# RWKV-7 layer of a two-layer trunk: one head per partition half, per-chunk transition matrices, a 16-wide inverse and LoRA inputs by linearity

## The chip, the cores and the metric

The kernel runs on one core of a Trainium2 chip. The metric is the device time of one execution in microseconds. The engines are TensorE (PE, with its weight loads PEld), VectorE (DVE), ScalarE (ACT), GpSimd (POOL) and SyncE (SP), which issues the DMAs.

## What is computed

A block of 512 tokens with 1024 channels goes through an RWKV-7 layer, an MLP, a differential-attention layer and a second MLP, each followed by a LayerNorm. Only the RWKV layer is touched by the change:

```python
xx = _token_shift(x) - x
xr, xw, xk, xv, xa, xg = (x + xx * mu[i] for i in range(6))   # written out in the source
r, k, v = xr @ w_r, xk @ w_k, xv @ w_v
w = -softplus(-(w0 + tanh(xw @ w1) @ w2)) - 0.5
a = sigmoid(a0 + (xa @ a1) @ a2)
g = sigmoid(xg @ g1) @ g2
kk = k * k_k;  kk = kk / max(norm(kk), 1e-12)                 # per head of 64
k = k * (1 + (a - 1) * k_a)
# per head, state S (64 x 64), 512 steps:
#   S_t = S_{t-1} diag(exp(-exp(w_t))) + (S_{t-1} a_t) b_t^T + v_t k_t^T ;  y_t = S_t r_t
y = _wkv7_scan(r, decay, k, v, -kk, kk * a)
y = layer_norm_per_head(y) + sum(r * k * r_k) * v
return (y * g) @ w_o
```

There are 16 heads of 64 channels. All data is float32.

## The kernel before

Dense products are made in three passes: each operand is split into a rounded high part (`split`, L101, a cast on ACT at L102) and a low part (a subtraction at L103, on POOL for the weights), and `mm3` (L134) multiplies high by high, high by low and low by high (L137 to L139). Weights come from DRAM in 256 KB pieces (`wst`).

The method `rwkv` first makes the LoRA inputs: DVE builds 24 mixed inputs (L262) from differences that POOL makes (L258), and PE multiplies them by the LoRA weights (L264). The mixed inputs of k, r and v follow in the same way (L245, L246). Then come the projections: k and r transposed, channels on partitions, with 512 columns, v with tokens on partitions and 256 columns. k also gives the squared norms (L300), whose inverse roots go through DRAM. The results go to DRAM and come back per pair of heads.

The sequence of 512 is cut into 8 chunks of 64. Heads are handled in 8 pairs p (128 channels) and 4 groups g of two pairs. For each pair `front` and `back` make decayed versions of r, k, a and b (the scan along time is L567; the products `ar` and `bk` are at L87, L599 and L600), and `amat` multiplies them into 64x128 blocks per chunk (L472), masks them on DVE (L474, L475) and transposes `bk` (L479). A triangular matrix of each chunk must be inverted: `inverse` writes the diagonal 32x32 blocks to DRAM (`nbD`), reads them back as `nu`, one block half on each partition (L503), and does a substitution of 31 steps with two operations each on DVE (L510 and L512; POOL for one group); the result goes out as `gbD` and comes back as `gt`. `inverse2` completes the 64x64 inverse with 32x32 matmuls (L535, L543). Then `chunk` runs 8 times for each of the 4 groups, and each run needs the state that the run before has left: 64x64 matmuls at L627 and L629, a copy, a product with the inverse (L632), a copy (L634), a product with the keys (L637), four scalings on DVE (L640), and products with the output matrix (L646). `finish` normalizes (L671 to L698), and the group's w_o product is added to the output rows (L407). A LayerNorm (L731 on; its transposes are L777) leads to the first MLP.

What runs when is set by three things: the `PLAN` string, which lists the steps of the RWKV layer in order (projections, F and B for front and back, A for `amat`, i and j for the inverse, s for a chunk, f for finish, w for w_o), priority offsets beside it (`PO`, `TP`), and the scheduler of the tile framework, which writes each engine's instructions in one order from this. DMAs are issued by SP in order. So the chunks of one group are woven with projections, the A blocks and the w_o products of others.

Of the kernel before, what the change touches and what calls it, by code (L numbers as in the profile page):

```python
# [8 lines left out]
F32 = mybir.dt.float32  # L9
# [9 lines left out]
P = 128  # L19
# [41 lines left out]
PO = {"k": [None, None, None, None], "r": [None, None, None, None], "v": [None, None, None, None], "F": [300, 300, 300, 300], "B": [300, 300, 300, 300], "A": [300, 300, 300, 300], "i": [600, 600, 600, 600], "j": [600, 600, 600, 600], "s": [0, 0, 0, 900], "f": [300, 300, 300, 1800], "l": [None, None, None, None], "c": [None, None, None, None], "w": [None, None, None, None], "n": [None, None, None, None]}  # L61
TP = {}


class Trunk:
# [102 lines left out]
    def rwkv(self):  # L168
# [5 lines left out]
        self.vD = self.t(self.dr, "vD", [T, D])  # L174
        self.rnD = self.t(self.dr, "rnD", [16, T])
        self.ssD = self.t(self.dr, "ssD", [4, 4, T])
        nbD = self.t(self.dr, "nbD", [4, 16, 4, 32, 32])
        gbD = self.t(self.dr, "gbD", [4, 16, 4, 32, 32])
        rp = self.pool("res", 1)
        self.psT = None  # L180
        with ExitStack() as ph:
            psA = self.pool("psA", 2, space=PSUM, ctx=ph)
            psE = self.pool("psE", 2, space=PSUM, ctx=ph)
            psB = self.pool("psB", 2, space=PSUM, ctx=ph)
            lp = self.pool("lora", 1, ctx=ph)
            ip = self.pool("inv", 1, ctx=ph)
            ep = self.pool("ew", 1, ctx=ph)
            ar_ = self.pool("arena", 4, ctx=ph)
            nbc = [0]
# [4 lines left out]
            xp = self.pool("xp", 1, side="right", ctx=xc)  # L194

            cvh = self.t(lp, "cvh", [P, 2, NK])
# [7 lines left out]
            self.rkb = self.t(lp, "rkb", [P, NK, 2])  # L204
# [7 lines left out]
            def big(tag, shape, dt=F32):  # L212
                if tag == "ba":
                    return self.t(rp, tag, shape, dt, bufs=4)
                if tag == "bc":
                    nbc[0] += 1
                    if nbc[0] % 4 in (1, 2):
                        return self.t(rp, "acc", shape, dt, bufs=2)
                    return self.t(ar_, "bc", shape, dt, bufs=2)
                return self.t(ar_, tag, shape, dt)  # L220

            l1 = big("ba", [P, NK, 256])
            lts = [big("ba", [P, 4, T]) for _ in range(2)]
            lts = [t[:, j] for t in lts for j in range(4)]
            xt = self.t(xp, "xt", [P, NK, T + 1])
            V.memset(xt[:, :, 0:1], 0.0)
            for c0, c1 in ((0, 1), (1, 2), (2, 4), (4, 6), (6, 8)):
                nc.sync.dma_start(out=xt[:, c0:c1, 1:T + 1], in_=a["xT"][:, c0:c1, :])
                nc.sync.dma_start(out=l1[:, c0:c1, :], in_=a["l1"][:, c0:c1, :])

            def mix(i, tag):
# [4 lines left out]
                for c in range(NK):  # L236
                    mix1(i, c, his[c], los[c], None, G if str(c) in (MRP if i == 0 else MVP) else V)
                return his, los

            def mix1(i, c, hi, lo, xx, E):  # L240
                tmp = self.t(xp, "tmp", [P, T], bufs=3)
                x0 = xt[:, c, 1:T + 1]
                if xx is None:
                    xx = tmp
                    G.tensor_tensor(out=xx, in0=xt[:, c, 0:T], in1=x0, op=ALU.subtract)  # L245
                V.scalar_tensor_tensor(out=tmp, in0=xx, scalar=cv[:, V_MU + i, c:c + 1], in1=x0, op0=ALU.mult, op1=ALU.add)  # L246
                self.split(hi, lo, tmp, E)

            pw = self.t(psB, "ch", [P, T])
            pa = self.t(psB, "ch", [P, T])  # L250
            pg = self.t(psB, "yy", [P, T])
            mk = [[big("bb", [P, 4, T], F32R) for _ in range(2)] for _ in range(2)]
            mk = [[z[c // 4][:, c % 4, :] for c in range(NK)] for z in mk]
            n = 0
            for c in range(NK):
                x0 = xt[:, c, 1:T + 1]
# [853 lines left out]
```

## Time and profile before

| | |
|---|---|
| median of three runs | 1532.91 us (1530.49 to 1537.92) |
| profiled execution, time | 1537.76 us |
| profiled execution, span | 1535.8 us |
| PE busy, share of the span | 92% |
| DVE, ACT, POOL busy | 54%, 37%, 28% |
| mean granted clock of PE | 0.931 |

The profile comes from one execution. A busy microsecond of PE is not one at full speed: the view of stretches gives the granted clock (PEclk) beside the busy time, 1.00 for 2.4 GHz and 0.5 for 1.2 GHz. The RWKV layer takes the first third of the span; the rest, two MLPs and the attention, is dense matmuls for the most part. The timelines give the start and the length of an instruction; a matmul in fp32 leaves two records, and a matmul's length includes its fill, so that starts of neighbours are nearer to each other than lengths.

### The profile page before, as it was taken

Reading aid. Unit: us, or ns where it says so; the run is one execution under the profiler, and the core shown is the slowest. Engines: PE = TensorE matmul, PEld = TensorE weight load, DVE = VectorE, ACT = ScalarE, POOL = GpSimd, SP = SyncE. Lnnn points to the kernel's source line nnn. Section 1 sums busy time; section 2 is a strip of 40 time slices with the busy share of each in tenths; the row PEclk is TensorE's granted clock in tenths of the full one; section 3 lists DMA queues with packets and bytes.
Section 4 is the critical chain, followed back from the end, with each engine's and each line's share of the span. In section 5 each row is a group of like instructions: output and inputs, shape, how many; then the busy total and the mean of one; then the engine's idle time right before and its main releaser. Section 6 shows DMA issues by size and latency. Waiting matters only on the chain.

```text
span 1535.8 us, 21834 instructions
## 1 busy us (share of the span) xinstructions
PE 1410.0 (92%) x8296; PEld 1151.9 (75%) x8296; DVE 829.9 (54%) x1668; ACT 561.0 (37%) x1074; POOL 430.6 (28%) x383
## 2 busy tenths in 40 slices
PE   7879888968899799999999989999988999999997
PEld 2547677847766598888888878888877988888886
DVE  8975475855876754333333553456667333333346
ACT  2333334143333362332314244566454413233220
POOL 5863333264335341010101144313232201010010
PEclk9889989755689999999999999999998999999999
DMA  5235463335131243333333035223112433333311
GB/s 163 69 125 146 122 146 103 97 77 132 54 96 42 96 138 111 96 96 97 97 99 93 28 102 158 76 76 110 62 64 74 138 96 96 96 96 96 96 42 55
DMA packets 89119, 148.14 MB, mean 96 GB/s; under 512 B 34312, under 2 KB 48040, under 8 KB 89016
## 3 DMA queue, kind: packets, MB, share of 16 engines
q1 hardware_dynamic: 89016, 146.76, 32.4%
q8 instruction: 65, 1.06, 0.3%
q14 instruction: 38, 0.31, 0.1%
HBM read 127.74 MB, written 10.57 MB: 90 GB/s over the span
## 4 chain that ended last, share of the span: by engine, by line
PE 72%; DVE 14%; DMA 7%; POOL 3%; ACT 2%; issue 2%; SPq 0%; DVEq 0%; ACTq 0%; POOLq 0%
PE a L137 11%; PE a L138 10%; PE a L139 10%; PE o L138 5%; PE o L139 5%; PE o L137 5%; PE s L138 5%; PE s L139 5%; PE s L137 5%; DMA nu<-nbD 3%; PE e L472 2%; DVE ba L262 1%; DMA gbD<-gu 1%; PE o L959 1%; DVE gtm L510 1%
## 5 line engine op out<-in xcount | busy, mean ns | idle before, releaser
L102 ACT CAST whi<-wst 128x1024 fp32r<-128x1024 f32 (+1 forms) x208 | 195.5, 952 | 354.8 <-PE a L139 146.4
L103 DVE TENSOR_TENSOR wlo<-wst,whi 128x1024 fp32r<-128x1024 f32 x120 | 149.6, 1247 | 223.7 <-ACT whi L102 223.7
L103 POOL TENSOR_TENSOR wlo<-wst,whi 128x512 fp32r<-128x512 f32 (+1 forms) x88 | 165.8, 1899 | 254.8 <-ACT whi L102 247.2
L87 POOL TENSOR_TENSOR r<-r 128x512 f32<-128x512 f32 x64 | 69.1, 1080 | 522.0 <-ACT hh L818 519.5
L137 PE MATMUL a<-ba,whi 128*128 128x512 f32 (+1 forms) x336 | 122.7, 366 | 2.7 <-DVE qT L907 2.2
L820 DVE TENSOR_TENSOR hl<-r,hh 128x512 fp32r<-128x512 f32 x64 | 45.8, 717 | 143.8 <-POOL r L87 143.8
L139 PE MATMUL a<-ba,wlo 128*128 128x512 f32 (+1 forms) x336 | 121.8, 363 | 0.0
L138 PE MATMUL a<-ba,whi 128*128 128x512 f32 (+1 forms) x336 | 121.7, 362 | 0.0
L139 PE MATMUL s<-ba,wlo 128*128 128x512 f32 (+1 forms) x232 | 81.3, 351 | 0.0
L138 PE MATMUL s<-ba,whi 128*128 128x512 f32 (+1 forms) x232 | 81.0, 349 | 0.0
L137 PE MATMUL s<-ba,whi 128*128 128x512 f32 (+1 forms) x232 | 80.8, 348 | 0.0
L137 PE MATMUL a<-whi,ba 128*128 128x256 f32 x256 | 76.0, 297 | 3.8 <-ACT ev L312 3.1
L138 PE MATMUL o<-ba,whi 128*128 128x512 f32 (+1 forms) x200 | 71.9, 359 | 3.6 <-DVE ba L103 3.6
L138 PE MATMUL a<-wlo,ba 128*128 128x256 f32 x256 | 74.9, 293 | 0.0
L137 PEld LDWEIGHTS a<-ba,whi 128*128 128x128 f32 x336 | 64.5, 193 | 13.7 <-issue 2.4
L139 PE MATMUL a<-whi,ba 128*128 128x256 f32 x256 | 74.5, 291 | 0.0
L137 PE MATMUL o<-ba,whi 128*128 128x512 f32 (+1 forms) x200 | 71.7, 359 | 1.3 <-ACT ba L102 1.3
L139 PE MATMUL o<-ba,wlo 128*128 128x512 f32 (+1 forms) x200 | 71.6, 358 | 0.0
L139 PEld LDWEIGHTS a<-ba,wlo 128*128 128x128 f32 x336 | 64.3, 192 | 9.5
L138 PEld LDWEIGHTS a<-ba,whi 128*128 128x128 f32 x336 | 64.6, 192 | 9.1
L137 PE MATMUL o<-whi,hh 128*128 128x512 f32 x176 | 68.7, 390 | 0.0
L138 PE MATMUL o<-wlo,hh 128*128 128x512 f32 x176 | 68.6, 390 | 0.0
(376 smaller groups left out, 3548.2 us busy)
## 6 DMA issues: line engine op xcount, KB each, us to landing
wst<-in_m SPq DMA_DIRECT2D x128, 512.0 KB, 3.9
wst<-in_kv SPq DMA_DIRECT2D x16, 512.0 KB, 3.8
wst<-in_wk SPq DMA_DIRECT2D x16, 256.0 KB, 4.2
wst<-in_wr SPq DMA_DIRECT2D x16, 256.0 KB, 3.4
wst<-in_wv SPq DMA_DIRECT2D x16, 256.0 KB, 3.8
wst<-in_q SPq DMA_DIRECT2D x8, 512.0 KB
kT<-kT SPq DMA_DIRECT2D x16, 256.0 KB, 3.3
wst<-in_wo SPq DMA_DIRECT2D x8, 512.0 KB, 3.3
```

Of the source, the lines that this page charges most:

```text
L87: return eng.tensor_tensor(out=out, in0=in0, in1=in1, op=ALU.mult)
L102: self.nc.scalar.copy(out=hi, in_=src)
L103: (lo_eng or self.nc.vector).tensor_tensor(out=lo, in0=src, in1=hi, op=ALU.subtract)
L137: mm(ps, lh, rh, start=first, stop=False)
L138: mm(ps, lh, rl, start=False, stop=False)
L139: mm(ps, ll, rh, start=False, stop=last)
L262: V.scalar_tensor_tensor(out=mx, in0=xx, scalar=cv[:, V_MU + i, c:c + 1], in1=x0, op0=ALU.mult, op1=ALU.add)
L472: PE.matmul(ps[:, c, :], d["bk"][hs, 4 * b + c].rearrange("p a t -> p (a t)"), d["ar"][hs, 4 * b + c].rearrange("p a t -> p (a t)"), start ...
L510: E.tensor_tensor(out=tmv, in0=GU[:, 0:m, s:s + 1].to_broadcast([P, m, n]), in1=NU[:, s:s + 1, s + 1:32].to_broadcast([P, m, n]), op=ALU.mult)
L820: V.tensor_tensor(out=hl, in0=r, in1=hh, op=ALU.subtract)
L959: PE.matmul(po[:, qb, :], at[:, kb, :], vt[:, kb, f * P:(f + 1) * P], start=(kb == 0), stop=(kb == qb))
```

## The change

The RWKV layer is rewritten; MLPs and attention stay.

- LoRA: the mixing is applied to the weights. POOL makes `ls = mu * l1` and `lx = l1 - ls` (three small products and one subtraction for each of 8 channel blocks), and PE adds `lx` times x and `ls` times the shifted x, two output blocks, 32 matmuls of 512 columns. The mixed inputs of k, r and v are made by ACT and DVE in PSUM.
- v is projected with channels on partitions like k and r. Norms are computed in two steps for eight heads each.
- The two heads of a pair lie on the two halves of the partitions (`H`). `amat` makes `am`, and copies `bn` and `an`.
- The inverse works on 16x16 blocks: 15 steps with two DVE operations, the 128 blocks of a group with one on each partition; `inverse2` widens them to 32 and 64 with 64x64 matmuls.
- `solve` makes for each chunk a transition matrix `mt` and an output matrix `rt` from the inverse, with six groups of sixteen 64x64 matmuls per pair.
- `scan` then carries the state: in each step one product `mt` times state is added in PSUM to a product that doesn't depend on the state, and DVE scales the sum into the next state.
- `finish` uses bn_stats for each chunk; the w_o step W(g) takes a whole group.
- The order is one string, without priority offsets. PSUM is 2 + 6 banks.

```diff
+PLAN = ("k0 r0 k1 r1 N0 k2 k3 N1 r2 r3 m v0 F0 A0 v1 F1 A1 v2 F2 v3 I0 x J0 J1 U0 U1 S0 A2 S1 F3 A3 Y0 Y1 "
+        "F4 I1 J2 J3 U2 U3 S2 A4 S3 F5 A5 Y2 Y3 W0 F6 I2 J4 J5 U4 U5 S4 A6 S5 F7 A7 Y4 Y5 W1 "
+        "I3 J6 J7 U6 U7 S6 S7 Y6 Y7 W2 W3")
...
+            def lora(c):
+                for i, c0, c1 in ((1, 0, 64), (4, 64, P), (5, P, 256)):
+                    G.tensor_scalar(out=ls[:, c, c0:c1], in0=l1[:, c, c0:c1], scalar1=cv[:, V_MU + i, c:c + 1],
+                                    scalar2=0.0, op0=ALU.mult, op1=ALU.add)
+                G.tensor_tensor(out=lx[:, c], in0=l1[:, c], in1=ls[:, c], op=ALU.subtract)
+                for ps, c0 in ((pwa, 0), (pg, P)):
+                    PE.matmul(ps, lx[:, c, c0:c0 + P], x0(c), start=(c == 0), stop=False)
+                    PE.matmul(ps, ls[:, c, c0:c0 + P], xs(c), start=False, stop=(c == NK - 1))
...
-                    PE.matmul(ps[r, :], l1[:, c, c0:c0 + r.stop - r.start], mx, start=(c == 0), stop=(c == NK - 1))
...
-        nc.sync.dma_start(out=NU.rearrange("p s t -> p (s t)"),
-                          in_=bass.AP(tensor=nb.tensor, offset=nb.offset, ap=[[0, 2], [1024, 64], [1, 1024]]))
-        for s in range(31):
-            n, m = 31 - s, s // 2 + 1
...
+        for q in range(2):
+            for h in range(2):
+                src = self.nbD[g, q, h]
+                r = 32 * (2 * q + h)
+                nc.sync.dma_start(out=NU[r:r + 32],
+                                  in_=bass.AP(tensor=src.tensor, offset=src.offset,
+                                              ap=[[16 * 65, 32], [64, 16], [1, 16]]))
+        for s in range(15):
+            n, m = 15 - s, s + 1
...
+        ps = self.bank((P, NCH, CH))
+        for c, h in HS:
+            PE.matmul(ps[H[h], c, :], w[H[h], c, :], bn[H[h], h, c, :], start=True, stop=True)
+        mt = self.t(cm, "mt", [P, NCH, CH], bufs=2)
+        V.tensor_tensor(out=mt, in0=ps, in1=cst[:, C_I2:C_I2 + CH].unsqueeze(1).to_broadcast([P, NCH, CH]), op=ALU.add)
...
+        for c in range(NCH):
+            ps = pc2[c % 2][:, c // 2, :]
+            if c < NCH - 1:
+                for h in range(2):
+                    PE.matmul(ps[H[h]], bn[:, h, c, :], uv[:, h, c, :], start=True, stop=(c == 0))
+            for h in range(2):
+                PE.matmul(py[H[h], c, :], am[:, h, c, 64:P], uv[:, h, c, :], start=True, stop=(c == 0))
+            if c:
+                if c < NCH - 1:
+                    for h in range(2):
+                        PE.matmul(ps[H[h]], mt[H[h], c, :], sc[H[h], c, :], start=False, stop=True)
+                for h in range(2):
+                    PE.matmul(py[H[h], c, :], rt[H[h], c, :], sc[H[h], c, :], start=False, stop=True)
+            if c < NCH - 1:
+                V.tensor_scalar_mul(sc[:, c + 1, :], ps, pc[:, c:c + 1])
...
-        for q, h in QH:
-            PE.matmul(ch[R[q], 0, h, :], ra[q][:, h, c, 0:CH], sv[q][:, h, :], start=True, stop=True)
-        for q, h in QH:
-            PE.matmul(yy[R[q], h, :], ra[q][:, h, c, CH:2 * CH], sv[q][:, h, :], start=(h == 0), stop=False)
-        S.copy(out=rs, in_=ch[:, 0])
-        for q, h in HQ:
-            PE.matmul(ch[R[q], 1, h, :], gf[R[q], 8 * h + c, :], rs[R[q], h, :], start=True, stop=True)
...
+        for c in range(NCH):
+            V.bn_stats(out=st[:, c, :], in_=py[:, c, :])
+            V.bn_aggr(out=mv[:, c, :], in_=st[:, c:c + 1, :])
```

The order on PE in the old chunk loop, in a stretch of group 1 (ch and yy are the PSUM tiles of the chunk, uv the values and state, acc, bc and bb its matrices, a the PSUM of another pair's A):

```order
L627 MATMUL ch_3313<-uv_3106,acc_1648 64x64
L629 MATMUL yy_3314<-uv_3106,acc_1648 64x64
L627 MATMUL ch_3313<-uv_3106,acc_1648 64x64
L629 MATMUL yy_3314<-uv_3106,acc_1648 64x64
L627 MATMUL ch_3313<-uv_3108,bc_1649 64x64
L629 MATMUL yy_3314<-uv_3108,bc_1649 64x64
L627 MATMUL ch_3313<-uv_3108,bc_1649 64x64
L629 MATMUL yy_3314<-uv_3108,bc_1649 64x64
L479 MATMUL a_2982<-cst_58,bk_2705 128x128 x4
L632 MATMUL ch_3313<-rs_3315,gf_2744 64x64 x4
L483 MATMUL a_2988<-rkb_112,r_484_2637 64x2 x8
```

The chunk's matmuls stood in small sets, woven with the A blocks of a later pair (L479, L483).

The order on PE where the new group 1 (pairs 2 and 3) begins its J and U (e is a PSUM bank, bb the A blocks `am`, tt the inverse, an and bc the copies of a, b and values):

```order
L528 MATMUL e_2607<-q_2605,bb_2112 64x64 x16
L534 MATMUL e_2626<-tt_2603,q_2624 64x64 x16
L541 MATMUL e_2646<-q_2644,bb_2112 64x32 x16
L548 MATMUL e_2665<-tt_2603,q_2663 32x32 x16
L528 MATMUL e_2691<-q_2689,bb_2291 64x64 x16
L534 MATMUL e_2710<-tt_2687,q_2708 64x64 x16
L541 MATMUL e_2730<-q_2728,bb_2291 64x32 x16
L548 MATMUL e_2749<-tt_2687,q_2747 32x32 x16
L564 MATMUL e_2770<-cst_58,vT_2768 64x64 x16
L569 MATMUL e_2789<-bc_2139,bb_2112 64x64
L574 MATMUL e_2808<-an_2177,tt_2603 64x64 x13
L569 MATMUL e_2789<-bc_2139,bb_2112 64x64 x15
```

The four J steps of one pair stand behind each other with no other row between, then those of the second pair, then U.

The order on DVE in the old inverse (gu is the inverse in the making, nu the block read back, t the decay sum of a front):

```order
L510 TENSOR_TENSOR gtm_1305<-gu_1280,nu_1282 128x96
L512 TENSOR_TENSOR gu_1280<-gu_1280,gtm_1305 128x4x24
L510 TENSOR_TENSOR gtm_1308<-gu_1280,nu_1282 128x115
L512 TENSOR_TENSOR gu_1280<-gu_1280,gtm_1308 128x5x23
L567 SCALAR_TENSOR_TENSOR t_270_1391<-cst_58,t_270_1391 128x512
L510 TENSOR_TENSOR gtm_1311<-gu_1280,nu_1282 128x110
L512 TENSOR_TENSOR gu_1280<-gu_1280,gtm_1311 128x5x22
L510 TENSOR_TENSOR gtm_1314<-gu_1280,nu_1282 128x126
```

And on DVE where the new inverse of group 1 begins (gr and gn belong to the finish of pair 0 or 1, nu is the block read back):

```order
L100 SCALAR_TENSOR_TENSOR gr_2454<-gr_2454,gv_2451 128x8
L101 SCALAR_TENSOR_TENSOR gr_2453<-gr_2454,gr_2453 128x8
L636 SCALAR_TENSOR_TENSOR gn_2465<-gmv_2434,gr_2453 128x8
L505 TENSOR_TENSOR gtm_2554<-gu_2548,nu_2547 128x15
L507 TENSOR_TENSOR gu_2548<-gu_2548,gtm_2554 128x15
L505 TENSOR_TENSOR gtm_2557<-gu_2548,nu_2547 128x28
L507 TENSOR_TENSOR gu_2548<-gu_2548,gtm_2557 128x2x14
L505 TENSOR_TENSOR gtm_2560<-gu_2548,nu_2547 128x39
L507 TENSOR_TENSOR gu_2548<-gu_2548,gtm_2560 128x3x13
```

The 31 steps of up to 136 columns have become 15 of up to 64, and they stand in DVE's order behind the statistics of both pairs of the group before.

## Rows read from the trace of the kernel before

**Rows 1.** PE's timeline, the first MLP: start us, us, instruction, its count, idle before.

```profile
531.52 0.28 PE L137 MATMUL s<-ba,whi 128*128 128x256 f32 x1
...
539.95 1.09 PE L777 MATMUL e<-cst,acc 128*128 128x128 f32 x4 [4.09 <-DVE lr L96]
```

**Rows 2.** Stretches: us; busy us (count) of PE, PEld, DVE, ACT, POOL; PEclk; DMA; GB/s.

```profile
250.00:300.00 50.00, 42.85 (x358) 36.15 (x357) 36.24 (x99) 12.51 (x31) 11.79 (x15) 0.84 0.38 105
300.00:350.00 50.00, 34.72 (x405) 27.97 (x403) 29.02 (x61) 20.63 (x46) 28.57 (x58) 0.62 0.28 68
350.00:400.00 50.00, 39.16 (x412) 33.36 (x412) 30.00 (x87) 14.31 (x38) 16.58 (x30) 0.52 0.40 104
...
450.00:500.00 50.00, 46.99 (x412) 33.74 (x410) 32.73 (x82) 17.42 (x46) 22.74 (x27) 0.99 0.14 40
```

**Rows 3.** PE's waits, 0 to 532 us: sum us, times, longest us.

```profile
PE e L300 <- ACT rnb L296: 13.9, 5, 7.6
```

**Rows 4.** The chain that ended last, longest pieces: start us, us, what.

```profile
166.08 14.53 DMA nu<-nbD
...
307.14 12.58 DMA gbD<-gu
...
359.65 3.21 DMA gbD<-gu
```

**Rows 5.** PE's timeline over one chunk step.

```profile
494.90 0.33 PE L627 MATMUL ch<-uv,bb 128*64 128x64 f32 x2
...
495.18 0.34 PE L627 MATMUL ch<-uv,bb 128*64 128x64 f32 x4
495.30 0.33 PE L629 MATMUL yy<-uv,bb 128*64 128x64 f32 x4
...
499.14 0.33 PE L627 MATMUL ch<-uv,bb 128*64 128x64 f32 x2
```

**Rows 6.** PE's groups of instructions, the LoRA matmuls: count, busy us, mean ns, idle.

```profile
L264 PE MATMUL ch<-ba,ba 128*64 128x512 f32 x32 | 16.6, 735 | 9.4 <-DVE ba L262 9.4
```

**Rows 7.** PE's timeline near 490 us, full clock.

```profile
490.13 0.45 PE L632 MATMUL ch<-rs,gf 64*64 64x64 f32 x8
490.50 0.50 PE L137 MATMUL a<-r,bc 128*128 128x512 f32 x1
...
491.31 0.39 PE L137 MATMUL a<-r,bc 128*128 128x512 f32 x1
491.54 0.39 PE L138 MATMUL a<-rnb,bc 128*128 128x512 f32 x1
```

**Rows 8.** PE's timeline near 363 us, half clock.

```profile
362.98 0.69 PE L632 MATMUL ch<-rs,gf 64*64 64x64 f32 x8
363.60 2.07 PE L472 MATMUL a<-ar,bk 64*128 64x128 f32 x8
```

**Rows 9.** DVE's groups of instructions, 0 to 532 us: busy us, mean ns, idle.

```profile
L640 DVE SCALAR_TENSOR_TENSOR uv<-ch,gpc,sps 64x64 f32<-64x64 f32 x96 | 23.6, 280 | 6.9 <-PE ch L637 3.4 <-PE yy L646 1.3 <-ACT bc L102 0.9
...
L567 DVE TENSOR_TENSOR_SCAN t<-cst,t 128x512 f32<-128x512 f32 x8 | 9.7, 1218 | 12.7 <-ACT t L566 12.7
...
L474 DVE TENSOR_TENSOR ba<-e,cst 64x512 f32<-64x512 f32 x8 | 5.5, 689 | 3.5 <-PE e L472 3.3
...
L672 DVE TENSOR_SCALAR gm<-gm 128x8 f32<-128x8 f32 x8 | 1.4, 186 | 0.1
```

**Rows 10.** ACT's groups of instructions, 0 to 532 us.

```profile
L480 ACT COPY bb<-e 128x512 f32<-128x512 f32 x4 | 2.4, 588 | 6.9 <-PE e L479 6.9
```

**Rows 11.** DVE's timeline in an inverse.

```profile
181.53 0.22 DVE L510 TENSOR_TENSOR gtm<-gu,nu 128x58 f32<-128x58 f32 x1
...
187.06 0.29 DVE L510 TENSOR_TENSOR gtm<-gu,nu 128x126 f32<-128x126 f32 x1
...
187.39 1.23 DVE L512 TENSOR_TENSOR gu<-gu,gtm 128x126 f32<-128x126 f32 x1
```

**Rows 12.** POOL's timeline in the same microseconds.

```profile
187.29 1.18 POOL L87 TENSOR_TENSOR ar<-rnb,e 128x512 f32<-128x512 f32 x1 [13.13 <-ACT e L571]
```

More of the change, by code (lines that the diff above doesn't have):

```diff
@@ L236, in mix @@
                 for c in range(NK):
-                    mix1(i, c, his[c], los[c], None, G if str(c) in (MRP if i == 0 else MVP) else V)
+                    mix1(i, c, his[c], los[c])
+                    if each is not None:
+                        each(c)
                 return his, los
[L240 to L247, printed above, removed]
@@ L344, in A @@
-            def A(p):
-                g, q = p // 2, p % 2
-                if q == 0:
-                    start(g)
-                gd = grp[g]
-                self.amat(pse, p, gd, el[p])
-                for half in range(2):
-                    r0 = 64 * q + 32 * half
-                    nc.sync.dma_start(out=nbD[g, :, 2 * q + half].rearrange("u s t -> s u t"),
-                                      in_=gd["ab"].rearrange("p h c t -> p (h c) t")[r0:r0 + 32, :, 32 * half:32 * half + 32])
@@ L355, in inv @@
-            def inv(g):
-                GU = self.t(ip, "gu", [P, 16, 32], bufs=2)
-                with tc.high_priority(offset=-(PO["i"][g] or 0)):
-                    nc.sync.dma_start(out=GU, in_=a["i32"])
-                self.inverse(ip, GU, nbD[g], gbD[g], G if str(g) in IPOOL else V)
-            def inv2(g):
-                self.inverse2(cm, ((psB, "ch"), (psB, "yy"), (psA, "a"), (psA, "a"))[g], gbD[g], grp[g])
-            pse = (psE, "e")
-            acc, wst, wos = [], {}, {}
-            def load(g):
-                if not acc:
+                nc.sync.dma_start(out=self.ssD[4 * g:4 * g + 4], in_=ss[0:4])
@@ L369, in load, with W @@
+            mr = mix(0, "bc")
+            el, tab = {}, {}
+            acc, wst = [], {}
+            def W(g):
+                if g == 0:
                     for i in range(2):
@@ L394, in wo @@
[L394 to L401 removed]
+                ws = []
@@ L402, in wo @@
+                for tt in range(NT):
                     for n in range(2):
@@ new lines, in inverse @@
+    def inverse(self, g):
+        nc, ep = self.nc, self.ep
+        V = nc.vector
+        NU = self.t(ep, "nu", [P, 16, 16])
+        GU = self.t(ep, "gu", [P, 16, 16])
+        nc.sync.dma_start(out=GU.rearrange("p s t -> p (s t)"), in_=self.a["i16"])
+        for q in range(2):
+            for h in range(2):
+                src = self.nbD[g, q, h]
[5 more added lines that the diff above has]
+            n, m = 15 - s, s + 1
+            tm = self.t(ep, "gtm", [P, 64], bufs=2)
+            tmv = tm[:, 0:m * n].rearrange("p (i t) -> p i t", t=n)
+            gv = GU[:, 0:m, s + 1:16]
+            V.tensor_tensor(out=tmv, in0=GU[:, 0:m, s:s + 1].to_broadcast([P, m, n]),
+                            in1=NU[:, s:s + 1, s + 1:16].to_broadcast([P, m, n]), op=ALU.mult)
+            V.tensor_tensor(out=gv, in0=gv, in1=tmv, op=ALU.add)
+        nc.sync.dma_start(out=self.gbD[g], in_=GU.rearrange("p s t -> p (s t)"))
```

682 lines of the change are left out of this document (310 added, 372 removed).

## The prediction, made before the changed kernel ran

> **What bounds the kernel now.** I read the table of stretches first, then TensorE's waits, then the chain that ended last, then single timelines for prices. The rest of the program, from the first MLP on, is the same code in both kernels, so only the time until the first MLP can run freely counts. In the kernel before, its first matmul starts at 531.52 us, but the engine later stands for 4.1 us until the last LayerNorm transposes at 539.95 [rows 1]; I count 541 us as the old end of the RWKV stage.
>
> TensorE is busy 35 to 47 us of every 50 in this stage [rows 2], but that hides two things. Between 300 and 400 us the granted clock is 0.62 and 0.52, so many of those busy microseconds are at the lower level, 1.2 GHz. And the engine rarely waits for long: the largest sum of waits at one line is 13.9 us, of L300 [rows 3]. The chain shows what stands behind that: the copy of the 32-wide blocks back from DRAM (`nu<-nbD`) takes 14.53 us, `gbD<-gu` 12.58 us [rows 4]. The old stage is a thread of latencies, filled rather well with projections and w_o matmuls of other groups. A chunk step of four heads starts at 494.90, the next at 499.14, 4.24 us, and there are 32 of these [rows 5].
>
> **The change part by part.**
>
> *LoRA and mixes.* Twenty-four mixed inputs vanish from DVE; in their place are 32 fp32 matmuls of 512 columns. One such matmul is two records; a record is 0.735 us long with its fill [rows 6], so a matmul lies between 0.735 and 1.47 us, and I take 0.95, as consecutive records overlap: 32 x 0.95 = 30 us, ending near 37 us. The old LoRA ended near the same place with projection matmuls already between, so this part gains little.
>
> *Projections.* Dense matmuls start 0.23 us apart [rows 7]. Twelve units of 48: 12 x 48 x 0.23 = 132 us. v now has 512 columns where it had 256, the same work. Norms 7 us, three fronts and two A-matrices between them 18 us, small waits 4: 37 + 132 + 7 + 18 + 4 = 198. The first inverse is mostly behind v2 and v3; with its last transfers J0 starts at 205.
>
> *Price of a group of sixteen 64x64 matmuls.* Eight records (four matmuls) of L632 occupy 490.13 to 490.50, 0.37 us [rows 7]; in a running stream four records start within 0.12 us (L627 at 495.18, the next at 495.30 [rows 5]), eight within 0.23, so sixteen matmuls take 0.37 + 3 x 0.23 = 1.06 us; 4 x 0.37 = 1.48 is the other bound. At the lower clock the eight take 362.98 to 363.60, 0.62 [rows 8], and sixteen, at twice 0.23 for each further eight, 2.0, 0.93 more. Of the 0.37, some 0.1 us stands beyond the 0.23 of the stream; it is paid where the work changes from dense tiles to quadrants. Some 100 such changes are 10 us if none is hidden; I count none of it, as the groups wait for DVE anyway. The Trainium skill ("TensorEngine Tiling (Array Packing)", Tiling Modes, Key Properties) says that a change of tiling mode drains the engine, which speaks against weaving 64x64 groups with other tiles; by that rule paid in full, the sum would be 10 us later, by the row's tenth it stays.
>
> *One pair's J.* Four groups (two only 32 columns wide), 4.0 us; on DVE a mask product and a sum from PSUM at 0.69 [rows 9] and a transpose at 0.7; an ACT copy at 0.59 [rows 10] and two half ones, 0.3 on the path; hops 0.3. Together 7.3, and the order has the pair's four groups in one row with nothing between, so two pairs take 14.6. *One pair's U.* Six groups, 6.4 us, with copies only partly covered by the parallel branch: 7 us, two pairs 14.
>
> *Scan, A, F, Y.* Here DVE sets the pace. Per group of two pairs: 14 scan scalings of 128x64 at 0.31 (a 64x64 from PSUM is 0.28 [rows 9]) 4.3; eight masks at 0.69 5.5; sixteen bn_stats at about 0.29 and sixteen bn_aggr at 0.2 7.8; two rsqrt chains, 24 small operations at 0.19 (128x8 is 0.186 [rows 9], which the bn_aggr follow too) 4.6; one front with its scan of 1.22 [rows 9] and five passes at 0.7 4.8. Sum 27.0; with the ramp of the first steps and hops 32 us. A scan step is short now (two PSUM accumulations, one DVE product), under 1 us against 4.24 for four heads before; but the group must wait for U and J first.
>
> *Inverse.* Thirty DVE operations of at most 64 elements at 0.24 (0.22 for 58 [rows 11]) 7.2 us, 2.8 more for a front's operations that stand between them in DVE's order. nbD out and back 4.5, gbD and dc 5. Bounds for the NU read, four transfers of 32 KB in 64-byte pieces: 1.6 us, half the 3.21 of gbD<-gu, which moves 128 KB, and 14.5, the old read [rows 4]; gbD<-gu, also many small pieces, is nearest, and I take 2.5. If it were the old one, +12 us for each of three groups. DVE work before and after the transfers, masks, products and transposes, adds 3.
>
> *One loop.* 14.6 + 14 + 32 + 4.5 + 7.2 + 2.8 + 5 + 3 = 83. W (48 dense matmuls, 11 us) lies in the idle time of the inverse. Three loops (groups 1 to 3), of which the last saves the A of a next group: 3 x 82 = 246.
>
> *Tail.* After U7: the scans 9, statistics and rsqrt of two pairs 12 (half of the 7.8 + 4.6 per pair is not enough: they follow each other), copies and transposes 5, W2 and W3 at 11 each, the LayerNorm of the last row blocks on DVE 14, and some 6 in which the first MLP weights' low parts stand behind LayerNorm operations in GpSimd's order: 68 us. *Removed without replacement:* the 14-us reads, the old chunk chain, the transposes of v.
>
> *Sum at full clock:* 205 + 29 (J0 to U1) + 246 + 68 = 548, against 541: +7. Two corrections. First, operations of DVE with two SBUF inputs stretch when GpSimd runs: beside a 1.18-us GpSimd operation the inverse's 128x126 took 1.23 instead of 0.29 [rows 11, 12]. About 3.5 us a group, 10 in all; the bounds are 0 and 10 for each group. The Trainium skill ("SBUF — State Buffer", Who interferes with whom) has a tensor_tensor with both inputs in SBUF contend with GpSimd's reads; by that rule, the trace agrees. Second, the clock. A loop holds twenty 64x64 groups with 0.93 each at stake, 18.6 us. In 250 to 300 us, a mix of dense and small work, the mean grant is 0.84, a third of the time at the lower level; in 300 to 400 it is 0.57, some 86% [rows 2]. The new group stage has less dense work than the former and more of it than the latter. I take a third, 6.2 a loop over three and a half loops, 22 us.
>
> So 548 + 10 + 22 = 580, 39 us later. The profiled execution is 1537.8 us, its span 1535.8 with 2 us around it: 1576.8. The median of the runs lies 4.9 us below the profiled one: **1572 us**.
>
> **The rivals.**
>
> *A: the loop is shorter, and the kernel faster.* If A and F of the next group finish under the first scan, so that NU's read and the inverse lie under the second scan and Y, a loop loses 12 us: 36 less. With the clock held and contention as taken, 541 - 548 + 36 - 10 = 19 us faster, 1514; with none of the contention 1504. For it: removed 14-us reads, and steps of under 1 us. Against: DVE carries 27 us in that stretch already, in one order.
>
> *B: the clock holds, the rest as forecast.* +17: 1550. For it: 450 to 500 us has 0.99 with chunk steps, though interleaved with dense matmuls [rows 2].
>
> *C: the clock stays low.* 86% of 18.6 over three and a half loops is 56, with the +17 a difference of 73 us: 1606. It decides from the point at which TensorE's busy share between inverses falls to that of 300 to 400 us. The Trainium skill ("TensorE: Matmul & The Clock Gate", What's actually happening) has activity release the lower level and idle bring it back; by that, C holds wherever the inverses leave TensorE idle, and 2.0 for 1.06 a group is what it costs.
>
> *D: about the same.* The +17 cancelled by 17 us of overlap that I don't see, 1533.
>
> **How the numbers follow.** Forecast 0.37, B 0.15, C 0.13, A 0.25, D 0.10. The range is 1508 to 1612, from the middle of A (half of its chance within) to C, with the NU read's upper bound partly outside. Half a per cent, 8 us, is about what a measurement of this kernel can tell from no change. Faster by more than that is 0.25 (A), within it 0.10 (D), slower 0.65 (the rest).
>
> **What would show it.** Right: in the new profile 64x64 groups at about 1.06 us at the full clock; J0 near 205, J2 near 290; first MLP matmuls near 580; a table of stretches in which TensorE is busy 25 to 35 us of 50 between 230 and 500 us with a grant of 0.7 to 0.9; DVE waiting some 3 us for NU. Wrong: a loop well under 75 us, inverse operations under scans, or a first MLP matmul before 530 (A); grants of 0.95 and more (B) or near 0.55 (C); a NU read of over 6 us. If matmuls of two partition halves don't run beside each other here as in the L632 rows, sixteen cost nearly double and all loops grow.

## The result, and the profile after

The changed kernel takes 1600.27 us (median of four, 1597.76 to 1603.74) against 1535.12 (four, 1530.49 to 1537.92) measured beside it: a ratio of 1.0429 [1.0393, 1.0465], 65 us slower. The forecast was 1572, slower, with 1606 as rival C. The profiled span grew by 62.1 us. From the first MLP on both kernels have the same code, so I put the whole growth ahead of it: the old end of the RWKV stage, 541 us, becomes 603.

The page of the changed kernel, the span and the busy times:

```profile
span 1597.9 us, 25151 instructions
PE 1440.1 (90%) x10200; PEld 1185.5 (74%) x10200; DVE 731.9 (46%) x1606; ACT 592.4 (37%) x1091; POOL 335.7 (21%) x260
```

The answer to [rows 2] is a table of stretches of the changed kernel, cut where its phases are: first one of the dense phase, then J and U of a group (odd rows) and the stretch between them with scans, statistics, fronts and the inverse (even rows), last the tail. The columns are those of [rows 2].

```profile
50.00:100.00 50.00, 50.00 (x209) 37.41 (x207) 7.94 (x16) 13.82 (x24) 21.06 (x17) 1.00 0.45 132
...
208.00:251.00 43.00, 29.25 (x648) 27.50 (x648) 8.07 (x12) 12.79 (x24) 9.53 (x8) 0.59 0.20 64
251.00:307.00 56.00, 36.73 (x464) 26.21 (x460) 40.72 (x134) 22.37 (x45) 10.24 (x7) 0.73 0.19 47
307.00:346.00 39.00, 30.05 (x650) 28.20 (x652) 8.05 (x12) 9.79 (x20) 1.27 (x1) 0.59 0.08 24
346.00:403.00 57.00, 44.71 (x494) 31.98 (x492) 41.72 (x137) 22.34 (x45) 9.84 (x7) 0.85 0.19 46
403.00:442.00 39.00, 31.03 (x668) 28.53 (x668) 10.25 (x17) 11.50 (x23) 6.30 (x5) 0.69 0.14 43
442.00:499.00 57.00, 46.32 (x500) 34.48 (x496) 39.86 (x132) 18.70 (x39) 10.29 (x8) 0.82 0.14 29
499.00:534.00 35.00, 26.59 (x647) 24.93 (x648) 7.18 (x11) 9.19 (x18) 0.00 (x0) 0.71 0.01 3
534.00:603.00 69.00, 49.32 (x431) 37.27 (x428) 47.15 (x170) 23.47 (x51) 13.28 (x10) 0.82 0.16 57
```

Two things are to be seen. The dense phase has the full clock and no idle time. The stages of J and U have grants of 0.59, 0.59, 0.69 and 0.71, although TensorE is busy for 68 to 80% of them. With levels of 1.2 and 2.4 GHz, a grant g means a share 2(1 - g) at the lower one: 82, 82, 62 and 58%, where the forecast took a third.

TensorE's timeline in J of the second group, pair by pair (start, length, tile, count, idle time before), answers [rows 7] and [rows 8]:

```profile
307.49 1.97 PE L528 MATMUL e<-q,bb 64*64 64x64 f32 x32 [0.91 <-DVE q L524]
310.35 1.98 PE L534 MATMUL e<-tt,q 64*64 64x64 f32 x32 [0.89 <-DVE q L530]
313.94 1.92 PE L541 MATMUL e<-q,bb 64*64 64x32 f32 x32 [1.62 <-DVE q L537]
316.43 1.07 PE L548 MATMUL e<-tt,q 64*32 64x32 f32 x32 [0.56 <-ACT q L543]
```

A group of sixteen takes 1.97 us where 1.06 was the price at the full clock and 2.0 at half. Before each stands a gap of 0.6 to 1.6 us for one DVE or ACT operation. The last group's J, behind a dense w_o product, shows the clock fall on the way: its first pair starts at the full level, its second runs at half.

```profile
498.92 1.15 PE L528 MATMUL e<-q,bb 64*64 64x64 f32 x32 [1.68 <-DVE q L524]
500.86 1.15 PE L534 MATMUL e<-tt,q 64*64 64x64 f32 x32 [0.78 <-DVE q L530]
...
506.00 1.97 PE L528 MATMUL e<-q,bb 64*64 64x64 f32 x32
```

TensorE's waits, 0 to 620 us (sum, times, longest), have two kinds where [rows 3] had L300's 13.9. L541 and L548 are gaps inside J. The long ones stand ahead of J: of L528's 14.8, 11.4 is the first J waiting for the first inverse, and L444 is a front's bonus matmul, whose 15.0 comes just before the second group's J (it ends its wait at 304.50, J starts at 307.49):

```profile
PE e L444 <- POOL in L90: 18.6, 4, 15.0
PE e L528 <- DVE q L524: 14.8, 4, 11.4
PE e L541 <- DVE q L537: 13.3, 8, 1.7
...
PE e L548 <- ACT q L543: 9.7, 8, 5.5
```

The chain that ended last has the read of NU (here the third group's) at 2.7 us, in place of the 14.53 in [rows 4]; DVE's timeline has the second group's inverse, first and last operation, 9.6 us, in place of the operations of [rows 11]:

```profile
378.10 2.40 DMA nbD<-bb
380.52 2.74 DMA nu<-nbD
```

```profile
289.31 0.17 DVE L505 TENSOR_TENSOR gtm<-gu,nu 128x15 f32<-128x15 f32 x1 [4.06 <-DMA g<-in_g]
...
298.71 0.18 DVE L507 TENSOR_TENSOR gu<-gu,gtm 128x15 f32<-128x15 f32 x1
```

By stages, in us (J+U: start of a group's J to the end of its U; U to J: from there to the next J):

| stage | forecast, full clock | measured |
|---|---|---|
| J0 starts | 205 | 208.4 |
| J+U, four groups | 4 x about 28.8 = 115 | 42.6, 38.3, 38.4, 35.1 = 154.4 |
| U to J, three times | 3 x 53.4 = 160 | 56.5, 57.4, 57.3 = 171.2 |
| tail after U7 | 68 | 69 |
| end of the stage | 548 (+10 contention, +22 clock: 580) | 603 |

### The profile page after: what moved, and what is told of

Read it like the earlier page. It is cut to its first block, busy times and chain, and to the rows that moved or that the text cites. A ratio compares the mean times of both kernels' runs of the same rounds, so it can differ in the third digit from the quotient of the medians.

```text
span 1597.9 us, 25151 instructions
## 1 busy us (share of the span) xinstructions
PE 1440.1 (90%) x10200; PEld 1185.5 (74%) x10200; DVE 731.9 (46%) x1606; ACT 592.4 (37%) x1091; POOL 335.7 (21%) x260
## 4 chain that ended last, share of the span: by engine, by line
PE 69%; DVE 11%; ACT 2%; DMA 2%; issue 1%; POOL 1%; SPq 0%; DVEq 0%; POOLq 0%; ACTq 0%
PE a L140 9%; PE a L141 8%; PE a L142 8%; PE o L141 5%; PE s L142 5%; PE o L142 5%; PE o L140 5%; PE s L141 5%; PE s L140 5%; PE o L913 1%; PE e L464 1%; PE e L579 1%; PE s L893 1%; PE e L528 1%; PE e L569 1%
## 5 line engine op out<-in xcount | busy, mean ns | idle before, releaser
L106 DVE TENSOR_TENSOR wlo<-wst,whi 128x1024 fp32r<-128x1024 f32 x120 | 147.9, 1233 | 228.2 <-ACT whi L105 228.2
L106 POOL TENSOR_TENSOR wlo<-wst,whi 128x512 fp32r<-128x512 f32 (+1 forms) x88 | 157.3, 1804 | 250.4 <-ACT whi L105 250.0
L140 PE MATMUL a<-ba,whi 128*128 128x512 f32 (+1 forms) x400 | 148.7, 372 | 4.8 <-DVE qT L861 2.2
L141 PE MATMUL a<-ba,whi 128*128 128x512 f32 (+1 forms) x400 | 147.2, 368 | 0.0
L142 PE MATMUL a<-ba,wlo 128*128 128x512 f32 (+1 forms) x400 | 146.8, 367 | 0.0
L140 PEld LDWEIGHTS a<-ba,whi 128*128 128x128 f32 x400 | 76.7, 192 | 20.0 <-issue 2.9
L142 PEld LDWEIGHTS a<-ba,wlo 128*128 128x128 f32 x400 | 76.7, 192 | 12.2
L141 PEld LDWEIGHTS a<-ba,whi 128*128 128x128 f32 x400 | 76.8, 192 | 11.5
L142 PE MATMUL o<-whi,hl 128*128 128x512 f32 x176 | 68.2, 390 | 0.0
L141 PE MATMUL a<-wlo,hh 128*128 128x512 f32 x168 | 65.4, 390 | 0.0
L140 PE MATMUL a<-whi,hh 128*128 128x512 f32 x168 | 65.4, 390 | 0.0
```

Of the source, the lines that this page charges most:

```text
L106: (lo_eng or self.nc.vector).tensor_tensor(out=lo, in0=src, in1=hi, op=ALU.subtract)
L140: mm(ps, lh, rh, start=first, stop=False)
L141: mm(ps, lh, rl, start=False, stop=False)
L142: mm(ps, ll, rh, start=False, stop=last)
```

## Experiments

All ratios are to the kernel before, whose median in these comparisons was 1535 to 1537 us. The theory: J and U hold the clock low, because a single pair's groups wait in turn for one DVE or ACT operation, and the missing time is there. The first rival: the missing time is in the stretch from U to the next J (DVE's sum, the inverse, transfers), and the clock is only an onlooker.

**e1: two pairs in step.** J and U become generators, and the groups of the two pairs are emitted alternately. Each pair has four scratch tiles instead of three `q` buffers shared by both.

```diff
+                elif op in "JU":
+                    f = {"J": self.inverse2, "U": self.solve}[op]
+                    if z % 2 == 0:
+                        for _ in zip_longest(f(z, el[z]), f(z + 1, el[z + 1])):
+                            pass
...
+        scr = d["scr"] = self.big("ba", [P, 4, NCH, CH])
...
-        tn = self.t(cm, "q", [P, NCH, CH], bufs=3)
+        tn = scr[:, 0]
```

> The J and U steps of a group's two pairs are written in step with each other (group of sixteen matmuls of the one pair, then the same group of the other), with scratch tiles of their own so that they can; nothing else moves. In the changed kernel J and U of a group take 38 us of TensorE's time line, twenty groups of 1.7 to 1.9 us at the half clock with gaps of 1 to 2 us between. Theory (the gaps let the clock fall, and the low clock is what the forecast undersized): with the gaps filled by the other pair's groups the granted clock returns within some 10 us, J and U take 24 to 28 us, and the kernel is 40 to 55 us faster than the changed one, 1545 to 1560. Rival 1 (64x64 groups hold the low clock however dense they stand): twenty groups of 1.9 us remain, 36 us, and the kernel gains at most 10 us, 1590 to 1600. Rival 2 (the time is lost outside J and U): no more than 10 us either, though J and U get shorter.

Measured: 1549.76 us, 1.0069 [1.0045, 1.0094], 50.5 less than the changed kernel. TensorE's timeline of e1 in the second group's J, and two rows of its table of stretches (J and U of the second and third groups):

```profile
289.76 3.44 PE L535 MATMUL e<-ba,bb 64*64 64x64 f32 x64 [2.11 <-DVE ba L531]
293.97 2.08 PE L542 MATMUL e<-tt,ba 64*64 64x64 f32 x64 [0.77 <-DVE ba L537]
```

```profile
289.80:313.50 23.70, 22.00 (x642) 21.20 (x642) 9.39 (x12) 11.78 (x23) 6.69 (x5) 0.86 0.27 83
...
373.40:399.00 25.60, 23.65 (x653) 21.73 (x652) 8.23 (x13) 11.44 (x22) 6.30 (x5) 0.93 0.21 65
```

The second batch of two groups takes 2.08 us, 1.04 a group, at the full clock. J+U are 23.2, 23.5, 25.6 and 28.5, together 100.8 instead of 154.4: 53.6 us, the whole gain. U to J stays: 57.5, 60.1, 55.4. The grants of the four are 0.89, 0.86, 0.93 and 0.82. So the theory holds for the place. What e1 can't do is part the clock from the gaps, since it removes both.

**e2: fillers in the gaps.** Nine 256-column matmuls whose result nobody reads stand between the groups of each pair's J; the gaps stay.

```diff
+        def fill(x, n):
+            for _ in range(n):
+                PE.matmul(wt[:, 0:256], cst[:, 0:P], x.rearrange("p c t -> p (c t)")[:, 0:256], start=True, stop=True)
...
+        fill(tn, 2)
...
+        fill(z1, 3)
```

> The changed kernel with 256-column matmuls on data at hand put behind the first three of the four J groups of each pair (two, three and four of them), into a PSUM tile that nobody reads: more work, in the gaps. Theory (the gaps let the clock fall): the granted clock in J and U rises from about 0.55 to over 0.85, the groups of J and U take 0.95 to 1.1 us again, and the kernel is 10 to 35 us faster than the changed one although it does more, 1565 to 1590. Rival 1 (64x64 groups hold the low clock): the added matmuls cost 0 to 10 us, 1600 to 1610, and the groups stay at 1.7 to 1.9 us.

Measured: 1587.39 us, 1.0321 [1.0301, 1.0341], 13 less, with more work than the changed kernel. Two stretches of e2, cut at the same times as in the changed kernel's table, and its TensorE timeline in the second group's J:

```profile
307.00:346.00 39.00, 34.44 (x749) 29.84 (x749) 12.36 (x20) 9.19 (x18) 1.27 (x1) 0.93 0.11 34
...
403.00:442.00 39.00, 36.27 (x817) 31.41 (x818) 11.54 (x21) 11.27 (x22) 6.30 (x5) 1.00 0.19 51
```

```profile
318.99 1.15 PE L534 MATMUL e<-q,bb 64*64 64x64 f32 x32
320.06 1.13 PE L529 MATMUL a<-q,cst 128*128 128x256 f32 x4
321.12 1.15 PE L541 MATMUL e<-tt,q 64*64 64x64 f32 x32
```

The grant rises from 0.59 and 0.69 to 0.93 and 1.00; over e2's own J and U (the second group's run from 308.8 to 341.8) it is 0.91, 0.95, 1.00 and 1.00. A group falls from 1.97 to 1.15 us and less. J+U sum to 137.7, 16.7 less. The fillers cost on the way: 18 a group, two records each, four records from 320.06 to 321.12, so 36 x 0.265 = 9.5 us a group, 38 in all, some of it in gaps. By this estimate the clock alone is worth between 16.7 and 16.7 + 38 = 55 us. The Trainium skill ("TensorE: Matmul & The Clock Gate", What's actually happening) has activity release the lower level and idle bring it back; the traces agree: 0.59 to 0.71 with the gaps, 0.82 to 1.00 with them filled, either by the other pair or by work without use. They agree in direction only: at the low grants TensorE was not idle but busy for 68 to 80% of the stretch.

**e3: without the substitution.**

```diff
-        for s in range(15):
+        for s in range(1):
```

> The changed kernel without fourteen of the fifteen substitution steps of each 16-wide inverse (28 DVE operations a group left out; its transfers stay). Theory (a group's stages follow one another, the inverse between Y and J on the path): the interval from the start of an inverse to J shrinks by 6 to 9 us in the three loops, in all 18 to 30 us, 1570 to 1582. Rival (it lies under a transfer, a front or w_o products): less than 5 us, 1595 to 1600.

Measured: 1589.55 us in one run, 10.7 less, between the two expectations. J0 starts 5.1 us earlier, and U to J is 55.0, 57.0 and 49.0 instead of 56.5, 57.4 and 57.3. Of some 9 us a group that DVE no longer spends, two loops show 1.5 and 0.4; only the last, whose inverse has no front beside it in the order, shows 8.3 (and J and U are 4 us longer in sum). In the first two the inverse isn't what sets the time from U to J. e3's trace shows what does. In the first loop TensorE waits 14.8 us at the bonus matmul of front F4, which stands in its order ahead of J, and J follows it:

```profile
295.66 2.07 PE L444 MATMUL e<-in,rkb 128*128 128x512 f32 x2 [14.76 <-POOL in L90]
297.66 1.97 PE L528 MATMUL e<-q,bb 64*64 64x64 f32 x32
```

In the second loop DVE has J's first input ready at 386.1, but J starts at 394.94, behind the w_o product W0 and F6's bonus matmul:

```profile
385.38 0.69 DVE L524 STREAM_TRANSPOSE q<-tt 128x512 f32<-128x512 f32 x1
```

```profile
394.00 1.02 PE L444 MATMUL e<-in,rkb 128*128 128x512 f32 x2
394.94 0.91 PE L528 MATMUL e<-q,bb 64*64 64x64 f32 x22
```

**e4: fronts and A ahead of the scans** (rival A made real, on e1). F3, F5, F7 stand before the scan; A is split, its masked products and the write of nbD early, its transposes (`b`) late.

```diff
-        ... J0 J1 U0 U1 S0 A2 S1 F3 A3 Y0 Y1 "
+        ... J0 J1 U0 U1 F3 S0 a2 S1 a3 b2 b3 Y0 Y1 "
```

> The first experiment, and besides the A blocks of the next group (matmuls, masks and the write for the inverse) stand before the end of the scans, apart from their transposes, with the second front ahead of the scans (its product tile has a buffer of its own): the inverse can begin while scan and statistics run. Theory (the next group's inverse waits for the front and A blocks that stand behind the scan): besides the gain of the first experiment each loop loses the 10 to 18 us from the end of the scans to the end of the inverse's first transfer, in all 30 to 50 us more, 1500 to 1530, faster than either kernel. Rival (DVE carries the stretch in any order): 0 to 10 us more than the first experiment, 1540 to 1560.

Measured: 1561.09 us, 1.0143 [1.0114, 1.0172], 11 slower than e1 where a gain was expected. TensorE's largest wait in e4 is at the front's bonus matmul (18.4 us in e1 from 200 to 520 us); three of the four, 7.4 us each, stand ahead of a scan that is ready:

```profile
PE e L453 <- POOL in L91: 32.8, 4, 10.6
```

The loops differ. U to J is some 74 us in the second, 14 more than in e1, though J's input is ready 12.5 us before J starts: W0 and F6's bonus matmul stand ahead of it again. In the third it is some 48, 7 less than in e1. The last J and U take 11 us more.

**e5: inputs earlier** (on e1): six `in` buffers instead of four, paid for with one w_o staging buffer and one `q` buffer fewer.

```diff
-        k32 = self.t(ep, "in", [P, T], bufs=4)
+        k32 = self.t(ep, "in", [P, T], bufs=6)
...
-                        s = self.t(cm2, "wst", [P, T], bufs=2)
+                        s = self.t(cm2, "wst", [P, T], bufs=1)
```

> The first experiment with six instead of four buffers for the three inputs of a front (the w_o staging and the finish give one buffer each for it); no step is moved. In the first experiment the front that stands between the two scans waits for its broadcast norms, whose transfer is issued only when the front before has let go of its buffers, 3.6 us on the chain of each loop, with DVE's passes behind it. Theory (the stretch from U to the next J is a chain of which the front's late inputs are a part): 3 to 6 us less in each of three loops, 1532 to 1542. Rival (A blocks and DVE's order set the stretch): less than 3 us in all, 1547 to 1551.

Measured: 1568.93 us, 1.0228 [1.0192, 1.0264], 19 slower than e1: both expectations missed. U to J is 55.7, 60.4, 57.0, as in e1. That doesn't clear the input loads, since the edit did not remove the wait that it was made for: DVE's wait for the broadcast norms, 200 to 520 us, is 4.0 in e1 and 11.8 in e5. The loss is in J and U (22.8, 29.5, 28.8, 34.8): ACT's waits in e5 show its queue held by casts of w_o that now wait for the one staging buffer, and TensorE's show J waiting for ACT's copies:

```profile
DVE in L430 <- DMA in<-rnD: 11.8, 4, 4.0
```

```profile
ACT ba L106 <- DMA wst<-in_wo: 36.5, 9, 4.8
```

```profile
PE e L558 <- ACT ba L552: 12.2, 4, 4.0
```

**e6: as e4, with the bonus matmul behind the scans.**

```diff
+        if "bon" not in d:
+            self.bonus(d)
         nu = self.big("bc", [P, 2, 2, NCH, CH])
```

> The fourth experiment (A blocks before the end of the scans) with one change: the fronts' bonus matmul, which waits for GpSimd's product of r and k, no longer stands in TensorE's order ahead of the scans but with the transposes behind them. Theory (in the fourth experiment TensorE stood 32.8 us at these matmuls with the ready scans queued behind them, and that ate the gain): 25 to 45 us less than the fourth, 1515 to 1535. Rival (DVE's 27 us of work for a group carry the stretch whatever the order): 0 to 10 us less, 1550 to 1560, no better than the first experiment.

Measured: 1575.58 us, 1.0268 [1.0237, 1.0298], 14 slower than e4: missed. The wait at the bonus matmul is gone, and U to J falls from some 181 us in e4 to 173, what e1 has, although the scan (L635) now stands for masks of A (`bb`), which are queued on DVE behind the early front's passes:

```profile
240.86 0.48 PE L635 MATMUL e<-bc 128*64 128x64 f32 x4 [5.01 <-DVE bb L480]
```

The loss is in J and U, some 22, 30, 29 and 43 us, 124 instead of e1's 101. In the second group J's mask (L553) comes to stand on DVE behind a front's passes (L443, L441, L442), and 10.6 us pass from J's first batch at 286.05 to its second:

```profile
292.36 1.74 DVE L441 TENSOR_TENSOR av<-in,av 128x512 f32<-128x512 f32 x1
...
295.84 0.68 DVE L553 TENSOR_TENSOR ba<-e,cst 128x512 f32<-128x512 f32 x1
```

**e7: e6 with e5's inputs.** The diff is that of e5 on e6.

> The sixth experiment with six buffers for a front's inputs as in the fifth. Theory: the front ahead of the scans starts without waiting, the next group's inverse begins under the second scan, and a loop falls from 81 us to 62 to 70: 1495 to 1520, faster than either kernel. Rival: as the sixth, 1515 to 1535, since the inputs lie under U then anyway.

Measured: 1589.73 us, 1.036 [1.0326, 1.0394]: missed again. It is 14 slower than e6; e5's edit cost 19 on e1.

**e8: W2 ahead of Y6** (on e1), in the scan pool's PSUM banks.

```diff
-        "I3 J6 J7 U6 U7 S6 S7 Y6 Y7 W2 W3")
+        "I3 J6 J7 U6 U7 S6 S7 W2 Y6 Y7 W3")
...
-                        ps = self.t(psA, "a", [P, T])
+                        ps = self.bank() if g == 2 else self.t(psA, "a", [P, T])
```

> The first experiment with the w_o product of group 2 written between the last scans and the last finishes, in banks of the pool that the scans use, so that its 48 dense matmuls fall between the scan steps of the last two pairs. In the first experiment TensorE is nearly idle from 491 to 503 us (the last statistics on DVE), and both last w_o products follow from 503.8 to 528.2. Theory (the tail is a chain, and dense work that is ready can stand beside its DVE part): 6 to 11 us less, 1539 to 1544. Rival (the additions to the output rows, eight of 0.74 us on DVE, push the statistics back by what TensorE gains): 0 to 4 us less, 1546 to 1551.

Measured: 1549.49 us, 1.0071 [1.0054, 1.0088], equal to e1. The woven matmuls stretch the last scans from 484.1-492.5 to 483.4-501.4 and put the first matmul of Y at 510.9 instead of 499.7; what W gains at the end, the scans have paid.

**e9: the first fronts ahead of their v projections** (on e1).

```diff
-PLAN = ("... m v0 F0 A0 v1 F1 A1 v2 F2 v3 I0 x J0 J1 ...
+PLAN = ("... m F0 v0 A0 F1 v1 A1 I0 v2 F2 v3 x J0 J1 ...
```

> The first experiment with the first two fronts and A blocks each one projection earlier and the first inverse ahead of the last two projections of v. In the first experiment v's last matmul is at 196.8 and J begins at 209.1, after the first inverse's last transfer. Theory (the first inverse can lie under v2 and v3): J begins at 198 to 202, 7 to 11 us less, 1539 to 1543. Rival (TensorE, whose order is fixed, now waits for the fronts that stand ahead of v0 and v1): as much is lost as gained, 1546 to 1554.

Measured: 1540.95 us (median of ten), 1.0031 [1.0017, 1.0044], 8.8 less than e1. The time is as expected, though J0 starts at 203.5, 5.6 earlier, and not at 198 to 202; the rest is in the loops, J to J 79.0, 79.2, 80.9 where e1 has 80.7, 83.6, 81.0 (e9's profile is that of its fastest run, 1535.39). This is the best version found; it is still not faster than the kernel before.

**e10: e8 and e9 together.**

> The eighth and ninth experiments in one. Theory: the two gains lie at different ends of the stage and add up, 13 to 22 us less than the first experiment, 1528 to 1537, level with the kernel before or a little faster. Rival: 0 to 6 us less, 1544 to 1550.

Measured: 1550.87 us, 1.0089 [1.0074, 1.0104], 10 slower than e9: missed. The two edits don't add.

**e11: I and J of the next group before Y, the front behind J** (on e9).

```diff
-        ... S1 F3 A3 Y0 Y1 F4 I1 J2 J3 U2 U3 ...
+        ... S1 F3 A3 I1 Y0 Y1 J2 J3 F4 U2 U3 ...
```

> The ninth experiment with the first front of the next group written after J instead of before the inverse, and the inverse ahead of the finishes. In the first and ninth experiments the front's five DVE passes and its scan stand between the end of the inverse and the first product of J (279 to 287 us in the first), partly while the inverse's result is on its way through DRAM. Theory (from U to the next J the time is set by DVE's order and by transfers between its pieces, not by one engine's sum): 2 to 4 us less in each of three loops, 1529 to 1535, level with or faster than the kernel before. Rival (the passes lie under the transfers, and behind J they delay U and the A blocks): the same or more, 1540 to 1552.

Measured: 1556.88 us, 1.0137 [1.012, 1.0154], 16 slower than e9 and above the range of either expectation. J starts at 203.5, 280.1, 372.1 and 462.0: the first loop is 2.4 us shorter than in e9, the next two 12.8 and 9.0 longer. The loss is in J and U of these two groups, some 34 us each where e9 has 22 and 24: the front's bonus matmul now stands between J and U, and TensorE waits 8.0 us for it in each.

```profile
298.94 2.08 PE L450 MATMUL e<-in,rkb 128*128 128x512 f32 x2 [8.01 <-POOL in L91]
```

**e12: one statistics pair instead of eight** (on e9; the means are of the wrong extent).

```diff
-        for c in range(NCH):
-            V.bn_stats(out=st[:, c, :], in_=py[:, c, :])
-            V.bn_aggr(out=mv[:, c, :], in_=st[:, c:c + 1, :])
+        V.bn_stats(out=st[:, 0, :], in_=py.rearrange("p c t -> p (c t)"))
+        V.bn_aggr(out=mv[:, 0, :], in_=st[:, 0:1, :])
+        V.tensor_copy(out=mv[:, 1:NCH, :], in_=mv[:, 0:1, :].to_broadcast([P, NCH - 1, 2]))
```

> The ninth experiment with one statistics operation per pair over all chunks, copied to the eight, in place of eight bn_stats and eight bn_aggr: 13 DVE operations a pair left out, some 2.5 us of DVE a pair, 5 a group; the normalization uses the wrong means. Theory (DVE's sum does not set the stretch from U to J; chains through TensorE, DVE and DRAM do): the loops lose under 2 us each and the tail 2 to 4, in all 2 to 8 us, 1533 to 1539. Rival (DVE's sum sets it): 4 to 5 us in each of three loops and 5 in the tail, 17 to 20 us, 1521 to 1524.

Measured: 1549.47 us, 1.0092 [1.0071, 1.0112], 8.5 slower than e9 with less DVE work: both expectations missed. Their price was wrong too: DVE's busy time in the whole program falls from 732.9 to 728.6 us, about 1 us a group and not 5, so e12 says little about DVE's sum. DVE's timeline of the third group's inverse in e12, then in e9:

```profile
346.11 0.17 DVE L511 TENSOR_TENSOR gtm<-gu,nu 128x15 f32<-128x15 f32 x1 [4.10 <-DMA nu<-nbD]
...
353.25 0.68 DVE L676 SCALAR_TENSOR_TENSOR acc<-acc,a 128x512 f32<-128x512 f32 x1
...
362.17 0.75 DVE L430 SCALAR_TENSOR_TENSOR in<-in,nkk,in 128x512 f32<-128x512 f32 x1 [1.04 <-DMA in<-rnD]
...
368.03 0.18 DVE L513 TENSOR_TENSOR gu<-gu,gtm 128x15 f32<-128x15 f32 x1
```

```profile
341.91 0.17 DVE L511 TENSOR_TENSOR gtm<-gu,nu 128x15 f32<-128x15 f32 x1 [3.72 <-DMA nu<-nbD]
...
350.80 0.18 DVE L513 TENSOR_TENSOR gu<-gu,gtm 128x15 f32<-128x15 f32 x1
```

The same thirty operations last 22.1 us in e12 and 9.1 in e9: with fewer statistics ahead, w_o additions (L676) and a front's passes, one of which waits for a load, come to stand between the steps of the inverse. U to J is some 68 us in this loop and 57 in e9. (The profiles, of e12's slowest run and e9's fastest, are 17 us apart, the medians 8.5.)

## Why the prediction was right, and where it was not

The direction was right, and so was the mechanism of J and U. From U to J the sum came out, but in part by luck. The long read went (2.7 us for 14.53, forecast 2.5), the scans became short (some 10 us for the last group's two pairs, 534.2 to 544.6, where eight steps of 4.24 us were 34), and what came in their place is what the sum named: J and U as chains, DVE's work, the inverse with its transfers.

- *Dense phase.* J0 at 208.4, forecast 205. The last v matmul ends at 196.2, forecast 198. Confirmed.
- *Inverse and DVE.* 9.6 us against 10; DVE is busy 40.7 us between U1 and J2, forecast 27 + 13 = 40. The sum is right and some of its terms are not: in the second loop the bn_stats and bn_aggr took 4.0 us where 7.8 was forecast, while the operations of finish and w_o on DVE (L106, L648, L649, L663), 6.9 us there, are not in the list.
- *U to J.* 171.2 against 160 + 10 for contention: right to 1 us. The path is not quite the forecast one. The sum has the inverse in series, but e3 took some 9 us out of it and two of three loops gained 1.5 and 0.4: the front's bonus matmul and the w_o product, ahead of J in TensorE's order, end at nearly the same time. That the sum met the longer of two such paths is luck.
- *Contention.* The trace has DVE operations beside GpSimd's that are 5.3, 3.4 and 4.2 us longer in the three loops than the shortest of their kind, 13 us for the forecast 10. How much of it reached J was not shown; no experiment took GpSimd's work away.
- *Tail.* 69 against 68.
- *J and U.* Forecast 115 + 22 = 137, measured 154.4: +17, the step that failed. The mis-sized term is "I take a third": it was 58 to 82%. At 18.6 us a group that is 2.84 x 18.6 = 53 us, close to the 56 of rival C; the rows show 39 over 115, so the 115 held up to 14 us of slack. The condition given for C, a low busy share between the inverses, was the wrong place. The grant there is 0.73 to 0.85; it is low in J and U themselves, where TensorE is busy most of the time, but in pieces with a gap before each. The rows that I averaged, [rows 2], mix dense work with chunk steps; none of them has such groups alone.
- *Sum.* 3.4 + 17 + 1 + 1 = 23 us, the stage's 603 against 580. The other 5 of the 28 between 1572 and 1600 come from the 4.9 us by which I put the median below the profiled execution; the changed kernel's median lies 0.6 above its profiled execution, 1599.71.

Of the rivals, A is answered in part. Giving the next group's A and front an earlier place cost 11, 26 and 40 us against e1 in three forms (e4, e6, e7; the last has e5's edit in it, which alone cost 19). What was moved came to stand ahead of a ready scan, or inside J and U, in the order of TensorE or DVE. No form also moved the w_o product and the front that stand ahead of J, so a shorter loop is not ruled out. B, 1550 with the clock held, is what e1 measured, 1549.8, though by other sums: J+U 14 below the full-clock estimate, U to J as in the changed kernel. D didn't occur.

**What stays open.** U to J is 55 to 60 us in the changed kernel, in e1 and in e5. The inverse's operations alone don't set it in two loops of three; there a front's bonus matmul and W0 hold J at nearly the same time. A kernel with these two behind J and all else unmoved was not run (e11 moved the front, and its bonus matmul then held U). The input loads and the statistics were not tested by e5 and e12, as said there. Nor is the exact part of the clock in J+U known, beyond the bounds of 16.7 and 55 us.

## What to carry to other kernels

Price a chain of small tile groups at the clock that its own gaps leave it, not at the mean of a mixed stretch, and emit independent chains in step, each with its own scratch: here that was worth 50 us of the 65 lost. Where a program decides the order, a shorter or earlier piece of work can put something else ahead of the critical one in an in-order queue, so look in the new trace for what now stands between the steps of the longest chain before trusting a saving.

## What the runs showed that was not expected

- TensorE at 77% busy was held at the lower clock for most of a stage (30.05 of 39 us busy, grant 0.59), when its work came in pieces of 1 to 2 us with gaps of 0.6 to 1.6; matmuls without use in the gaps raised the grant to 0.93 and the kernel became 13 us faster.
- About 1 us less DVE work a group made the kernel 8.5 us slower (e12), and the same 30 operations stretched from 9.1 to 22.1 us. Some of the stretch is longer operations: in e12's trace an inverse step of 0.23 us took 1.21 beside a GpSimd operation, as in [rows 11] and [rows 12]; DVE's row, then GpSimd's:

```profile
352.12 1.21 DVE L513 TENSOR_TENSOR gu<-gu,gtm 128x63 f32<-128x63 f32 x1
```

```profile
352.03 2.35 POOL L91 TENSOR_TENSOR ar<-in,e 128x512 f32<-128x512 f32 x2 [18.22 <-ACT e L428]
```
